# Two wide products first, then two narrow ones, in the weights-stationary projections of a decoder trunk

## The chip, the cores and the metric

The kernel runs on one core of a Trainium2 chip. The metric is device time in microseconds; the time before is the median of three runs. A profiled execution of the same program gives the trace that is read below.

The engines have the names of the profile: PE is the matrix engine (PEld its weight loads, which overlap its products), DVE and ACT are the two engines that work on whole tiles with 128 partitions, POOL and SP issue transfers here. A product (MATMUL) streams its moving operand, up to 512 columns, past a stationary one of 128 by 128 that a weight load (LDWEIGHTS) has put into PE before. It adds into an accumulator in PSUM. One PSUM tile of 128 partitions by 512 floats holds one accumulator.

## The reference

Four decoder layers on 256 tokens of 2048 features. Layer by layer the mixer is latent attention, sparse attention, sliding-window attention, and latent attention again. Each layer is one branch on a normalized input:

```
h = rmsnorm(x, norm_in[i])
self_out, mq, gate = mixer(h, w_in, ...)          # h @ w_in gives all streams
mem_out = memory_attention(mq, mem_n @ w_mem_kv[i])
y = concat(self_out, mem_out) * silu(gate)
x = x + y @ w_out[i]
```

and a last RMSNorm follows. All arrays are float32. Nearly all the arithmetic is in the products with weights: `w_in` (2048 by some 6700 to 7200), `w_mem_kv` (2048 by 2048), `w_out` (3072 by 2048), and in the latent layers `w_uq` and `w_ukv`.

## The kernel before

**High and low parts.** PE takes the operands in a rounded float32 form. To keep accuracy each operand is held as a high part, rounded, and a low part, the remainder. A product then is the sum of high times high, high times low and low times high. Activations are split once when they are made: `xT`, `cT` and `mT` hold for each block of 128 features a tile of 2 x 256 columns, the high parts of 256 tokens and then the low ones. Weights are split as they arrive: `stage` (L200) loads a tile `wr` with SP, and `parts_of` (L216) makes `wh` on ACT (the copy at L60) and `wl` on DVE (the subtraction at L64), 512 columns at a time, three buffers each.

**Two ways to multiply.** `rows_by` (L222) has the activations stationary and streams the weights: per weight row (128 features) and block of 128 tokens three products of up to 512 columns, L234 to L236. It makes values, the query and key streams that need rows, and the output projection. `columns_by` (L239), the function that is changed, has the weights stationary: the result comes out transposed, features on partitions. It works on 256 output features at a time, as two tiles `acc[0]` and `acc[1]` of 2 x 256 columns. Per weight row `kt` and tile `j` there are two products. The wide one (L253) has `wh` stationary and streams the high and the low part of the activations, 512 columns, over the whole accumulator. The narrow one (L255) has `wl` stationary and streams the high part alone, 256 columns, over the first half of the same accumulator. The halves are added when the accumulator is read: by `total` (L259) or `head_parts` (L265), with ACT and DVE.

A pair of `wh` and `wl` holds two weight rows (`k` is 0 or 1) of 256 columns, so eight products use one pair. A group, that is one call, has 16 weight rows for the input projections (`acc_g` gates, `acc_mq` memory queries, `acc_cq` the low-rank queries) and for the memory keys (`acc_mk`), 12 for `acc_qn` and 4 for `acc_kn`. PSUM holds four accumulators for products with weights (tag "acc"), so the group after next writes over the accumulators of this one.

**What sets the order.** The kernel is written for a planner: each engine's instructions are put into a fixed sequence beforehand by a plan that goes through the program with modelled durations. An instruction earlier in the program goes first, unless what it needs is not ready in the plan; then a later one that is ready takes its place. The sequence on PE therefore follows the source in general, with products of the attention of the previous part in between, and differs where an operand comes late in the plan. On the chip the engines run these fixed sequences and wait for each other with semaphores.

Memory keys and values of all four layers come first (up to some 400 us), then the four layers; in each the projections of one part are interleaved with the attention and the output projection of the part before.

Of the kernel before, what the change touches and what calls it, by code (L numbers as in the profile page):

```python
# [15 lines left out]
P = 128  # L16
S = 256
# [14 lines left out]
def kernel(ctx: ExitStack, tc: tile.TileContext, a: dict, out: bass.AP,  # L32
# [167 lines left out]
    def stage(w, k0, m, cols):  # L200

        n = cols[1] if len(cols) == 2 else cols[1] * cols[4]
        wr = wp.tile([P, ST * 512], F32, name="wr", tag="wr", bufs=WR)
        src = w[k0 * P:(k0 + m) * P, :].rearrange("(k p) n -> p k n", p=P)
        dst = wr[:, :m * n].rearrange("p (k n) -> p k n", k=m)
        if len(cols) == 2:
            nc.sync.dma_start(dst, src[:, :, cols[0]:cols[0] + n])
        else:
            c0, r, step, off, width = cols
            for k in range(m):  # L210
                nc.sync.dma_start(dst[:, k, :].rearrange("p (r c) -> p r c", r=r),
                                  src[:, k, c0:c0 + r * step].rearrange("p (r c) -> p r c", r=r)
                                  [:, :, off:off + width])
        return wr, n

    def parts_of(wr, c0, n):  # L216
        wh = wp.tile([P, 512], F32R, name="wh", tag="wh", bufs=3)
        wl = wp.tile([P, 512], F32R, name="wl", tag="wl", bufs=3)
        split(wh[:, :n], wl[:, :n], wr[:, c0:c0 + n])
        return wh, wl  # L220
# [18 lines left out]
    def columns_by(xt, kts, w, k0, cols, name):  # L239

        acc = [ps.tile([P, 2, S], F32, name=f"acc_{name}{j}", tag="acc", bufs=4) for j in range(2)]
        for s in range(0, kts, 2 * ST):
            m = min(2 * ST, kts - s)
            wr, n = stage(w, k0 + s, m, cols)
            for k2 in range(0, m, 2):
                wh, wl = parts_of(wr, k2 * S, 2 * S)
                for k in range(2):
                    kt = s + k2 + k
                    q = xt[kt // 4]
                    first, last = kt == 0, kt == kts - 1  # L250
                    for j in range(2):
                        o = k * S + j * P
                        nc.tensor.matmul(acc[j], wh[:, o:o + P], q[:, :, kt % 4, :],  # L253
                                         start=first, stop=False)
                        nc.tensor.matmul(acc[j][:, 0, :], wl[:, o:o + P], q[:, 0, kt % 4, :],  # L255
                                         start=False, stop=last)
        return acc

    def total(acc, name="z"):  # L259
# [47 lines left out]
    def memory():  # L307
# [19 lines left out]
        for i in range(depth):  # L327
            w = a["w_mem_kv"][i]
            for p_ in range(2):
# [11 lines left out]
                for h in (2 * p_, 2 * p_ + 1):  # L341
                    acc = columns_by(mT, 16, w, 0, (h * 256, 256), "mk")
                    kT = act.tile([P, 2, 2, S], F32R, name="mkT", tag="pq", bufs=PQ)
                    for j in range(2):
                        z = total(acc[j])
                        zs = wk.tile([P, S], F32, name="zs", tag="z", bufs=3)
                        nc.vector.tensor_mul(zs, z, mbc)
                        split(kT[:, 0, j, :], kT[:, 1, j, :], zs)
                    nc.gpsimd.dma_start(mkT[i][h], kT)
# [22 lines left out]
    def gate(nm, w, c0):  # L372
        gT = act.tile([P, 4, S], F32, name="gT", tag="gT", bufs=2)
        for h in range(2):
            acc = columns_by(nm.at, 16, w, 0, (c0 + h * S, S), "g")
            for j in range(2):
                z = total(acc[j])
                hz = wk.tile([P, S], F32, name="hz", tag="z", bufs=3)
                nc.vector.tensor_mul(hz, z, nm.half)
                th = wk.tile([P, S], F32, name="th", tag="e", bufs=4)  # L380
                nc.scalar.activation(th, hz, AF.Tanh)
                nc.vector.scalar_tensor_tensor(gT[:, 2 * h + j, :], th, 1.0, hz, op0=OP.add, op1=OP.mult)
        return gT
# [65 lines left out]
    def memory_project(nm, i, w, mq0, g0, part):  # L449
        kT, qT = [], []  # L450
        v = [act.tile([P, 2, 512], F32R, name="mvr", tag="aux", bufs=AUX) for z in range(2)]
        for z in range(2):
            nc.gpsimd.dma_start(v[z], mv[i][part][:, z])
        for h in range(2):
            k = act.tile([P, 2, 2, S], F32R, name="mkr", tag="pq", bufs=PQ)
            nc.gpsimd.dma_start(k, mkT[i][2 * part + h])
            kT.append(k)
            acc = columns_by(nm.at, 16, w, 0, (mq0 + part * 512 + h * 256, 256), "mq")
            q = act.tile([P, 2, 2, S], F32R, name="mqT", tag="pq", bufs=PQ)
            head_parts(q, acc)  # L460
            qT.append(q)
        return nm, kT, v, qT, gate(nm, w, g0 + 2048 + part * 512)
# [435 lines left out]
```

## Time and profile before

| | |
|---|---|
| Median of 3 runs | 2647.21 us (2645.34 to 2647.49) |
| Profiled execution | 2644.4 us, its span 2642.5 us |
| PE busy | 2614.7 us, 14623 products |
| PEld busy | 2268.1 us, 14623 weight loads |
| DVE busy, ACT busy | 1900.3 us, 1627.2 us |
| Mean granted PE clock | 0.998 |

The span goes from the first to the last instruction of the profiled execution. Busy is the union of an engine's instructions. Products overlap, each begins before the one ahead has ended, so what a product costs is read as the step from its start to the next one's start, not as its duration. The product rows L253 and L255 are those of the changed function.

### The profile page before, as it was taken

How to read it: one execution, taken by the hardware profiler on the slowest of the kernel's cores; microseconds unless marked ns; L12 is line 12 of the kernel's file. 1: busy time of each engine (PE TensorE's matmuls, PEld its weight loads, DVE VectorE, ACT ScalarE, POOL GpSimd, SP SyncE). 2: the span in 40 equal slices, each digit the busy share in tenths (PEclk: the TensorE clock that was granted, in tenths of full speed). 3: DMA queues.
4: the chain of work that ended last, by engine and by line, in shares of the span. 5: the costliest groups of instructions: out<-in, count | busy, mean ns of one | idle time of the engine just before them, and what ended most of it. 6: DMA issues, size and time to landing. Idle time of an engine off the chain costs nothing.

```text
span 2642.5 us, 43005 instructions
## 1 busy us (share of the span) xinstructions
PE 2614.7 (99%) x14623; PEld 2268.1 (86%) x14623; DVE 1900.3 (72%) x4174; ACT 1627.2 (62%) x3460; POOL 57.8 (2%) x102
## 2 busy tenths in 40 slices
PE   8999999999999999999999999999999999999998
PEld 7788888888888888888888888888888888888886
DVE  7566656677777786877777776777778767777767
ACT  6455556566656566666666666666666656665555
POOL 1000000000000000000000000000000000000000
PEclk9999999999999999999999999999999999999999
DMA  7888887565557655555556565555555756655763
GB/s 266 273 269 270 278 262 209 160 191 161 171 164 216 191 191 168 170 184 173 172 166 193 189 191 177 169 175 180 189 166 164 203 163 188 165 170 153 224 184 134
DMA packets 454065, 507.51 MB, mean 192 GB/s; under 512 B 69300, under 2 KB 352180, under 8 KB 452692
## 3 DMA queue, kind: packets, MB, share of 16 engines
q1 hardware_dynamic: 439716, 446.42, 55.5%
q0 software_dynamic: 13120, 56.17, 6.7%
q8 instruction: 115, 1.88, 0.3%
q10 hardware_dynamic: 1008, 2.16, 0.2%
q14 instruction: 106, 0.87, 0.1%
HBM read 485.70 MB, written 31.56 MB: 196 GB/s over the span
## 4 chain that ended last, share of the span: by engine, by line
PE 97%; DMA 2%; DVE 1%; ACT 0%; issue 0%; ACTq 0%; POOLq 0%
PE acc_g L253 14%; PE acc_g L255 7%; PE acc_wo L234 7%; PE acc_wo L235 7%; PE acc_wo L236 7%; PE acc_mq L253 5%; PE acc_mk L253 5%; PE acc_qn L253 3%; PE acc_cq L253 3%; PE acc_mq L255 2%; PE acc_mk L255 2%; PE acc_q L234 2%; PE acc_q L235 2%; PE acc_q L236 2%; PE acc_mv L235 2%; PE acc_mv L234 2%
## 5 line engine op out<-in xcount | busy, mean ns | idle before, releaser
L64 DVE TENSOR_TENSOR wl<-wr,wh 128x512 fp32r<-128x512 f32 (+2 forms) x1776 | 1171.6, 663 | 609.7 <-ACT wh L60 577.7
L60 ACT ACTIVATE wh<-wr 128x512 fp32r<-128x512 f32 (+2 forms) x1776 | 1080.5, 609 | 809.6 <-PE acc_g L253 172.4
L253 PE MATMUL acc_g<-xT,wh 128*128 128x512 f32 x1536 | 518.8, 398 | 0.0
L255 PE MATMUL acc_g<-xT,wl 128*128 128x256 f32 x1536 | 374.2, 282 | 0.0
L255 PEld LDWEIGHTS acc_g<-xT,wl 128*128 128x128 f32 x1536 | 287.5, 189 | 28.0
L235 PE MATMUL acc_wo<-wl,y 128*128 128x512 f32 x768 | 303.6, 395 | 0.8 <-DVE wl L64 0.8
L236 PE MATMUL acc_wo<-wh,y 128*128 128x512 f32 x768 | 298.6, 390 | 0.0
L253 PEld LDWEIGHTS acc_g<-xT,wh 128*128 128x128 f32 x1536 | 265.2, 188 | 36.4
L234 PE MATMUL acc_wo<-wh,y 128*128 128x512 f32 x768 | 240.7, 393 | 0.6 <-ACT wh L60 0.6
L253 PE MATMUL acc_mq<-xT,wh 128*128 128x512 f32 x512 | 173.2, 397 | 0.0
L253 PE MATMUL acc_mk<-mT,wh 128*128 128x512 f32 x512 | 171.4, 397 | 0.0
L235 PEld LDWEIGHTS acc_wo<-wl,y 128*128 128x128 f32 x768 | 144.3, 188 | 29.7 <-DVE wl L64 1.6
L236 PEld LDWEIGHTS acc_wo<-wh,y 128*128 128x128 f32 x768 | 144.3, 188 | 27.9
L234 PEld LDWEIGHTS acc_wo<-wh,y 128*128 128x128 f32 x768 | 141.7, 188 | 28.9 <-ACT wh L60 0.8
L805 DVE TENSOR_TENSOR x<-x,acc_wo 128x512 f32<-128x512 f32 x192 | 126.2, 681 | 12.3 <-PE acc_wo L236 12.1
L253 PE MATMUL acc_qn<-cT,wh 128*128 128x512 f32 x384 | 129.6, 398 | 0.0
L253 PE MATMUL acc_cq<-xT,wh 128*128 128x512 f32 x384 | 127.8, 395 | 0.0
L255 PE MATMUL acc_mq<-xT,wl 128*128 128x256 f32 x512 | 126.5, 285 | 0.0
L255 PE MATMUL acc_mk<-mT,wl 128*128 128x256 f32 x512 | 123.0, 282 | 0.0
L255 PEld LDWEIGHTS acc_mk<-mT,wl 128*128 128x128 f32 x512 | 96.6, 189 | 10.8
L235 PE MATMUL acc_q<-wl,xT 128*128 128x512 f32 x256 | 102.4, 400 | 0.0
L235 PE MATMUL acc_mv<-wl,mT 128*128 128x512 f32 x256 | 100.8, 394 | 0.3 <-DVE wl L64 0.3
(284 smaller groups left out, 4533.9 us busy)
## 6 DMA issues: line engine op xcount, KB each, us to landing
wr<-in_w_out_dram SPq DMA_DIRECT2D x192, 512.0 KB, 3.7
wr<-in_w_in_a_dram SPq DMA_DIRECT2D x176, 512.0 KB, 3.8
wr<-in_w_mem_kv_dram SPq DMA_DIRECT2D x128, 512.0 KB, 4.7
wr<-in_w_in_b_dram SPq DMA_DIRECT2D x112, 512.0 KB, 3.4
wr<-in_w_in_c_dram SPq DMA_DIRECT2D x104, 512.0 KB, 3.5
wr<-in_w_uq_dram SPq DMA_DIRECT2D x288, 128.0 KB, 2.7
tab<-flat POOLq DMA_DIRECT2D x8, 1536.0 KB, 11.0
wr<-in_w_in_a_dram SPq DMA_DIRECT2D x32, 288.0 KB, 3.2
```

What stands on the lines that cost most here:

```text
L60: nc.scalar.activation(o, i, AF.Copy, scale=scale)
L64: nc.vector.tensor_sub(lo, src, f32(hi))
L234: nc.tensor.matmul(acc[t][:, :n], xh, wh[:, :n], start=first, stop=False)
L235: nc.tensor.matmul(acc[t][:, :n], xh, wl[:, :n], start=False, stop=False)
L236: nc.tensor.matmul(acc[t][:, :n], xl, wh[:, :n], start=False, stop=last)
L253: nc.tensor.matmul(acc[j], wh[:, o:o + P], q[:, :, kt % 4, :], start=first, stop=False)
L255: nc.tensor.matmul(acc[j][:, 0, :], wl[:, o:o + P], q[:, 0, kt % 4, :], start=False, stop=last)
L805: nc.vector.tensor_add(xs, xs, acc[t])
```

## The change

Before, the two products of the first tile (wide, narrow) were written ahead of the two of the second tile (wide, narrow). After, the wide products of both tiles are written first and then both narrow ones. Operands, accumulators and the number of instructions are the same. The `start` and `stop` flags stay with the first wide and the last narrow product of each accumulator.

```diff
                 for k in range(2):
                     kt = s + k2 + k
                     q = xt[kt // 4]
-                    first, last = kt == 0, kt == kts - 1
+
                     for j in range(2):
                         o = k * S + j * P
                         nc.tensor.matmul(acc[j], wh[:, o:o + P], q[:, :, kt % 4, :],
-                                         start=first, stop=False)
+                                         start=kt == 0, stop=False)
+                    for j in range(2):
+                        o = k * S + j * P
                         nc.tensor.matmul(acc[j][:, 0, :], wl[:, o:o + P], q[:, 0, kt % 4, :],
-                                         start=False, stop=last)
+                                         start=False, stop=kt == kts - 1)
```

## The prediction

> **What bounds the kernel now.** I read the page first (span, busy shares, the chain that ended last), then the waits of PE, then the groups of instructions, and last the timeline of PE.
>
> ```profile
> span 2642.5 us, 43005 instructions
> PE 2614.7 (99%) x14623; PEld 2268.1 (86%) x14623; DVE 1900.3 (72%) x4174; ACT 1627.2 (62%) x3460; POOL 57.8 (2%) x102
> PE 97%; DMA 2%; DVE 1%; ACT 0%; issue 0%; ACTq 0%; POOLq 0%
> ```
>
> PE is busy for 99% of the span and carries 97% of the chain, so the time is the sum of the steps from one product's start to the next one's start. The waits of PE say how much of it is something else; the columns are who waited, for what, the total in us, how often, and the longest.
>
> ```profile
> PE gp L91 <- DMA rows<-in_mem_norm_dram: 7.6, 1, 7.6
> PE acc_mv L234 <- ACT wh L60: 3.2, 2, 2.9
> PE acc_kvb L234 <- ACT wh L60: 2.3, 1, 2.3
> PE acc_wo L235 <- DVE wl L64: 0.8, 2, 0.5
> ```
>
> Beside the first load (7.6 us) PE waits for 3.2 + 2.3 + 0.8 us and two smaller rows. Neither the splits nor the transfers set the pace. So the change is worth what it does to the step between products, and nothing else unless it makes a new wait.
>
> The groups give the number of products it touches. L253 is the 512-column product (I write W, wide), L255 the 256-column one (N, narrow):
>
> ```profile
> L253 PE MATMUL acc_g<-xT,wh 128*128 128x512 f32 x1536 | 518.8, 398 | 0.0
> L253 PE MATMUL acc_mq<-xT,wh 128*128 128x512 f32 x512 | 173.2, 397 | 0.0
> L253 PE MATMUL acc_mk<-mT,wh 128*128 128x512 f32 x512 | 171.4, 397 | 0.0
> L253 PE MATMUL acc_qn<-cT,wh 128*128 128x512 f32 x384 | 129.6, 398 | 0.0
> L253 PE MATMUL acc_cq<-xT,wh 128*128 128x512 f32 x384 | 127.8, 395 | 0.0
> L253 PE MATMUL acc_kn<-cT,wh 128*128 128x512 f32 x128 | 44.3, 397 | 0.0
> ```
>
> 1536 + 512 + 512 + 384 + 384 + 128 = 3456 wide products, and as many narrow ones. A weight row takes two of each, a quad: 1728 quads. The means of 398 ns are not steps: the products overlap, and what one costs has to be read from start to start.
>
> That is in the timeline of PE: start, length of the merged row, and "x2" where two products of one kind stand next to each other. The first stretch is an early one, the second is the last of the run:
>
> ```profile
> 44.35 0.64 PE L253 MATMUL acc_mk<-mT,wh 128*128 128x512 f32 x2
> 44.83 0.40 PE L255 MATMUL acc_mk<-mT,wl 128*128 128x256 f32 x2
> 45.06 0.40 PE L253 MATMUL acc_mk<-mT,wh 128*128 128x512 f32 x1
> ...
> 45.76 0.62 PE L253 MATMUL acc_mk<-mT,wh 128*128 128x512 f32 x2
> ...
> 2578.32 0.40 PE L253 MATMUL acc_g<-xT,wh 128*128 128x512 f32 x1
> 2578.55 0.28 PE L255 MATMUL acc_g<-xT,wl 128*128 128x256 f32 x1
> 2578.67 0.40 PE L253 MATMUL acc_g<-xT,wh 128*128 128x512 f32 x1
> 2578.91 0.28 PE L255 MATMUL acc_g<-xT,wl 128*128 128x256 f32 x1
> 2579.03 0.62 PE L253 MATMUL acc_g<-xT,wh 128*128 128x512 f32 x2
> 2579.49 0.40 PE L255 MATMUL acc_g<-xT,wl 128*128 128x256 f32 x2
> 2579.72 0.40 PE L253 MATMUL acc_g<-xT,wh 128*128 128x512 f32 x1
> ```
>
> The reader is to see that the source says W N W N, and yet every second quad of the program already runs as W W N N. I read it so: the planner took the second wide product where the low part wl was not ready in its plan: that is the first row of each pair of weight rows; in the second row of the pair both parts are there and the order is the written one. At 2579.03 the W W N N quad takes 0.69 us (to 2579.72), the W N W N quad before it 0.71 (2578.32 to 2579.03). Over the whole timeline I counted 620 undisturbed W W N N quads (those that start at 44.35 and 2579.03 are the first and the last), of mean 695.6 ns, and 790 undisturbed W N W N quads, of mean 707.8 ns. Counted with the disturbed ones, 815 quads have their two wide products side by side, 913 have not.
>
> **The change part by part.** It removes and adds no instruction, no transfer and no wait: 3456 products of each kind, 6912 weight loads and all the splits stay. Three things move.
>
> *The order in a quad.* 913 quads go from 707.8 to 695.6 ns: 913 x 12.2 ns = 11.1 us, all on PE and all on the path. The unknown in it: in the trace no two W W N N quads stand next to each other, each has a W N W N one before it. The rows that bound the pace of W W N N in an unbroken row are these, long runs of one kind and long runs of the alternating order:
>
> ```profile
> 700.66 0.62 PE L234 MATMUL acc_wo<-wh,y 128*128 128x512 f32 x2
> 702.02 0.62 PE L234 MATMUL acc_wo<-wh,y 128*128 128x512 f32 x2
> ...
> 2182.28 0.28 PE L235 MATMUL acc_qr<-wl,cT 128*128 128x256 f32 x1
> 2182.88 0.40 PE L253 MATMUL acc_qn<-cT,wh 128*128 128x512 f32 x1
> ...
> 895.33 0.40 PE L253 MATMUL acc_mq<-xT,wh 128*128 128x512 f32 x1
> 898.86 0.64 PE L253 MATMUL acc_mq<-xT,wh 128*128 128x512 f32 x2
> ...
> 1148.81 0.39 PE L253 MATMUL acc_g<-xT,wh 128*128 128x512 f32 x1
> 1150.55 0.62 PE L253 MATMUL acc_g<-xT,wh 128*128 128x512 f32 x2
> ```
>
> Six wide products of the rows loop take 702.02 - 700.66 = 1.36 us, 227 ns each; five narrow ones 0.60 us, 120 ns each. A quad made of these is 2 x (227 + 120) = 694 ns. The alternating order runs ten pairs in 3.53 us at 895.33 (706 ns a quad), but five pairs in 1.74 us at 1148.81 (696 ns). So there are two paces, some 694 and some 707 to 713, and the same order is found at both. The slow one is met by 641 of the 790 alternating quads and by 30 of the 620 others, of which 44.35 to 45.06 is one, at 0.71 us. Bounds for the new order: 693 ns below (the fastest quads of either order), 713 above. I take 695.6, since 589 of 620 quads of this order have it within 5 ns, whatever came before them.
>
> A page would have it otherwise. The Trainium skill, "TensorE: Matmul & The Clock Gate", section "Back-to-back issue gap", gives a warm step of N/2.4 + 2.5 ns, hence an estimate of 2 x (215.8 + 109.2) = 650 ns for a quad in any order, and a change worth 0 us. The trace disagrees with it on both counts, with 0.69 and 0.71 us for the two orders; it stays as a rival below.
>
> *The end of a group.* After sixteen weight rows (twelve, or four) the two accumulators are read out. The first was complete before the last W N; now it is complete one wide product later, 0.23 us. ACT and DVE, which read it, start 0.23 us later, and the splits queued behind those reads on both engines may shift with them. The accumulator is written again by the group after next, a whole group of some 11 us (16 x 702 ns) later where it has 16 rows. The short key groups are the place without such cover:
>
> ```profile
> 738.62 0.41 DVE L271 TENSOR_TENSOR qn<-zl,acc_qn 128x256 fp32r<-128x256 f32 x1
> ...
> 739.02 0.40 PE L253 MATMUL acc_kn<-cT,wh 128*128 128x512 f32 x1
> ```
>
> The last read of acc_qn ends at 739.03 and the wide product into that buffer starts at 739.02: released just in time. There are 8 such pairs of groups, and the value group behind each I count as just as near. At 16 places by at most 0.23 us this costs 3.7 us; below nothing it can't go, since nothing is freed earlier. I take 0.8 us, about a quarter, as the planner may put a narrow product first where the second accumulator is late.
>
> *When the parts come free.* The last use of wh in a pair moves ahead by one narrow product, 0.12 us, so ACT may begin the split after next by so much earlier; wl is freed as before. PE waits for splits in a few rows above only, so this is worth 0. No queue is passed: SP and POOL issue what they issued, by the same releases. The gain of the first 400 us, about 128 quads x 12.2 ns = 1.6 us, could be eaten by the waits for loads in that stretch (3.2 and 2.3 us above) if those end at a fixed time; I take 0, as the loads are released by PE's own progress, and keep 1.6 for the range.
>
> Sum: 11.1 - 0.8 = 10.3 us. The profiled execution took 2644.4 us (span 2642.5), so 2634.1, or 0.9961 of it. The median of the three runs, 2647.21, is 2.8 us above the profiled one; times 0.9961 it is 2636.9.
>
> **The rivals.** All quads together now average (815 x 695.6 + 913 x 707.8) / 1728 = 702.0 ns, and 0.2% of the time, about what a measurement of this kernel can tell from no change, is 5.3 us or 3.1 ns a quad.
>
> *The order does nothing.* The two paces belong to a state of PE's pipeline, not to the order: 1148.81 shows the written order at 696 ns, 44.35 the new one at 710. At 44.35 the slow W W N N is followed by a fast W N W N (45.06 to 45.76 in the same view), so that the eight products take the same 1.41 us as those from 2578.32 to 2579.72 (1.40). The 567 undisturbed eights of this kind, of which these are the first and, shifted by a quad, the last, have a mean of 1405.4 ns, 555 of them between 1400 and 1410. If eight products cost that whatever their order, a quad stays at 702 and the time at 2647. The same comes out if the planner kept its old order. Against it: 589 of 620, and 641 of 790. The skill's formula above would also end here.
>
> *Slower.* W W N N quads in an unbroken row lock into the slow pace, as the alternating ones do at 895.33. The price is in the row at 44.35: 713 ns for each of 1728 quads, 1728 x (713 - 702.0) = 19 us, 2666. It decides from a mean above 705.1. For it: the case was never seen, and what comes before a quad does matter in 30 of 620. Against it: the runs of one kind at 227 and 120 ns have no slow pace.
>
> **How the numbers follow.** My forecast has 0.70, with a range of its own of 2632 to 2641.9: below from 693 ns a quad (1728 x 9 = 15.6 us less), above the 0.2% bound, which 3.7 us at the group ends and 1.6 us of the early stretch still leave (11.1 - 5.3 = 5.8). No change has 0.16, slower 0.14. The range for all reaches from 2631 into the case of no change, to 2649, which leaves about 2 in 10 out, most of it the slower case.
>
> **What would show it.** In the changed kernel's timeline nearly every weight row should read "L253 x2", "L255 x2", and one such quad should take 0.69 to 0.70 us from start to start; a full gate group, 16 quads of which 8 change, should fall by about 0.1 us. PE's waits should stay below 10 us beside the first load. If the quads read 0.70 to 0.71 in an unbroken row, the order alone was not the cause; if the order is right and the quads are fast but the time is not down by 10 us, the loss is in new waits for ACT or DVE at acc_kn and acc_va, or for loads before 400 us.

## The result, and the profile after

The changed kernel takes 2637.05 us (median of 6 runs) against 2646.06 us before (median of 6): a ratio of 0.9964, with a 95% interval from 0.9954 to 0.9974. Measured once more later, beside another experiment, the ratio was 0.9975 (0.9965 to 0.9984). So 0.25 to 0.36% went, some 6 to 10 us; the two intervals together allow 0.16 to 0.46%. The prediction had 2636.9 us; its sum, 10.3 us, is at the upper end of that, and the reason it gave for it was only half right.

The profiled execution has a span of 2635.0 us, 7.5 less than before. From the page of the changed kernel:

```profile
span 2635.0 us, 43048 instructions
PE 2605.1 (99%) x14623; PEld 2260.1 (86%) x14623; DVE 1890.2 (72%) x4174; ACT 1625.5 (62%) x3460; POOL 57.8 (2%) x102
```

PE still sets the time, with the same 14623 products. The waits of PE in the changed kernel (who, for what, us in total, times, longest):

```profile
PE gp L91 <- DMA rows<-in_mem_norm_dram: 7.2, 1, 7.2
PE acc_kvb L234 <- ACT wh L60: 1.8, 1, 1.8
PE o L786 <- ACT pT L60: 1.7, 3, 0.6
PE acc_mk L253 <- ACT wh L60: 1.4, 1, 1.4
PE ptp L402 <- ACT e L60: 1.4, 3, 0.5
```

The waits have mostly moved: the 3.2 us at acc_mv are nearly gone, and 1.4 us at acc_mk and 3.1 us in the attention (o, ptp) have come. All rows behind the first load make some 9 us now and 7 before. There is no wait at acc_kn, where the prediction had looked for one.

The timeline of PE, in a gate group of the changed kernel (L257 is the narrow product here):

```profile
743.48 0.63 PE L253 MATMUL acc_g<-xT,wh 128*128 128x512 f32 x2
743.95 0.39 PE L257 MATMUL acc_g<-xT,wl 128*128 128x256 f32 x2
744.18 0.62 PE L253 MATMUL acc_g<-xT,wh 128*128 128x512 f32 x2
...
747.66 0.63 PE L253 MATMUL acc_g<-xT,wh 128*128 128x512 f32 x2
```

Every quad now reads "x2", "x2". Six of them take 747.66 - 743.48 = 4.18 us, 696.7 ns each. Counted over the whole trace, 1359 undisturbed quads (with products of this function ahead of them, behind them and throughout) run in this order, of mean 697.0 ns. 68 quads still alternate, 32 of them in acc_kn, where the planner has kept W N W N. A full gate group takes 11.14 us now and took 11.25.

I added up the steps from each product's start to the next one's. The wide and narrow products of `columns_by` take 1216.34 us after and 1223.57 before: 7.2 us less. All other products take 1398.1 us after and 1397.9 before, but only in the sum. Part by part they moved both ways: acc_mv takes 3.5 us less and acc_wo 1.8 less, o takes 3.2 us more and ptp 2.8 more. These shifts come with the new plan; they stand within 0.6 us in the second profile of the changed kernel, and they cancel. What is left of the difference lies in the changed products, as a shorter step.

### The profile page after: what moved, and what is told of

Read it like the earlier page. It is cut to its first block, busy times and chain, and to the rows that moved or that the text cites. A ratio compares the mean times of both kernels' runs of the same rounds, so it can differ in the third digit from the quotient of the medians.

```text
span 2635.0 us, 43048 instructions
## 1 busy us (share of the span) xinstructions
PE 2605.1 (99%) x14623; PEld 2260.1 (86%) x14623; DVE 1890.2 (72%) x4174; ACT 1625.5 (62%) x3460; POOL 57.8 (2%) x102
## 4 chain that ended last, share of the span: by engine, by line
PE 97%; DMA 1%; DVE 1%; ACT 0%; issue 0%; ACTq 0%; POOLq 0%
PE acc_g L253 14%; PE acc_g L257 7%; PE acc_wo L234 7%; PE acc_wo L235 7%; PE acc_wo L236 7%; PE acc_mq L253 5%; PE acc_mk L253 5%; PE acc_qn L253 3%; PE acc_cq L253 3%; PE acc_mq L257 2%; PE acc_mk L257 2%; PE acc_q L234 2%; PE acc_q L235 2%; PE acc_q L236 2%; PE acc_mv L235 2%; PE acc_mv L236 2%
## 5 line engine op out<-in xcount | busy, mean ns | idle before, releaser
L253 PE MATMUL acc_g<-xT,wh 128*128 128x512 f32 x1536 | 488.9, 397 | 0.6 <-DVE z L264 0.6
L257 PEld LDWEIGHTS acc_g<-xT,wl 128*128 128x128 f32 x1536 | 285.2, 188 | 60.7
L257 PE MATMUL acc_g<-xT,wl 128*128 128x256 f32 x1536 | 311.0, 280 | 0.0
L253 PEld LDWEIGHTS acc_g<-xT,wh 128*128 128x128 f32 x1536 | 238.1, 189 | 4.7 <-issue 1.1
L253 PE MATMUL acc_mk<-mT,wh 128*128 128x512 f32 x512 | 160.8, 396 | 1.4 <-ACT wh L60 1.4
L253 PE MATMUL acc_mq<-xT,wh 128*128 128x512 f32 x512 | 161.7, 397 | 0.0
L253 PE MATMUL acc_qn<-cT,wh 128*128 128x512 f32 x384 | 123.2, 399 | 0.0
L253 PE MATMUL acc_cq<-xT,wh 128*128 128x512 f32 x384 | 120.8, 396 | 0.0
L257 PEld LDWEIGHTS acc_mk<-mT,wl 128*128 128x128 f32 x512 | 95.8, 188 | 22.7 <-DVE wl L64 0.4
L257 PEld LDWEIGHTS acc_mq<-xT,wl 128*128 128x128 f32 x512 | 93.7, 188 | 20.0
L257 PE MATMUL acc_mq<-xT,wl 128*128 128x256 f32 x512 | 102.5, 281 | 0.0
L257 PE MATMUL acc_mk<-mT,wl 128*128 128x256 f32 x512 | 100.8, 278 | 0.0
```

## The experiments

The theory on record was that each quad (four products of one weight row) has a price by its own order: 707.8 ns alternating, 695.6 two and two. Its rival was that the two paces are a state of PE, with eight products at 1405 ns in any order. Two more could be named as reasons for a price by order: each change of width costs, or each product that writes the accumulator its predecessor has just written costs.

### Alternating everywhere

```diff
-                        nc.tensor.matmul(acc[j], wh[:, o:o + P], q[:, :, kt % 4, :],
-                                         start=first, stop=False)
+                        wide = nc.tensor.matmul(acc[j], wh[:, o:o + P], q[:, :, kt % 4, :],
+                                                start=first, stop=False)
+                        if j == 1:
+                            tc.keep_in_program_order(wide)
```

This is the kernel before, with the second wide product of a row pinned behind the first narrow one.

> The order of before, but each second wide product is pinned behind the first narrow one, so that the planner can't put two wide products side by side: nearly all 1728 quads run W N W N. If the order of widths sets the pace (707.8 ns for W N W N, 695.6 for W W N N in the trace of before), the 815 quads that stood as W W N N lose 12.2 ns each: 9.9 us, 2656 us, ratio to before about 1.0038. If the two paces are a state of PE and eight products cost 1405 ns in any order, the time stays at 2646 (ratio 1.000) and the quads average 702. If an unbroken alternating order finds the fast pace (694, as at 1148.81 us in the trace of before), the kernel is faster than before: 1728 x 8 ns = 14 us, 2632.

Measured: 2645.99 us against 2645.36, a ratio of 1.0004 (0.9995 to 1.0013). Hardly a quad is two and two any more, and yet nothing is lost. The undisturbed quads have a mean of 702.7 ns, but that is a mean of long stretches at one of two paces. (A single quad of the slow stretches takes 711 or 699 ns, so a pace has to be read over many.) From the timeline of PE in this kernel, the ends of two stretches of 15 quads each:

```profile
88.42 0.40 PE L253 MATMUL acc_mk<-mT,wh 128*128 128x512 f32 x1
...
99.02 0.40 PE L253 MATMUL acc_mk<-mT,wh 128*128 128x512 f32 x1
...
2570.13 0.39 PE L253 MATMUL acc_g<-xT,wh 128*128 128x512 f32 x1
...
2580.53 0.39 PE L253 MATMUL acc_g<-xT,wh 128*128 128x512 f32 x1
```

The first takes 10.60 us, 706.7 ns a quad, the second 10.40 us, 693.3, with a granted clock of 1.00 in both. So the alternating order has no price of its own: it is the fastest order or a slow one. The theory on record falls in this form; the 707.8 ns were those of alternating quads behind a W W N N.

### The narrow products in the other order

```diff
-                    for j in range(2):
+                    for j in (1, 0):
                         o = k * S + j * P
                         nc.tensor.matmul(acc[j][:, 0, :], wl[:, o:o + P], q[:, 0, kt % 4, :],
```

> The changed kernel with the two narrow products of a row exchanged: W0 W1 N1 N0. The widths follow each other as in the changed kernel, but twice in a quad a product goes into the accumulator that the one ahead of it has just written (W1 N1, and N0 before the next W0), as it did in W N W N. If the change of width is what costs, quads stay at 697 ns and the time at 2637 (ratio 0.9965). If writing the same accumulator twice running is what costs, quads go to about 708 and the time to about 2656 (ratio 1.004).

Measured: 2637.83 us, ratio 0.9973 (0.9963 to 0.9982), undisturbed quads of mean 697.0 ns, as in the changed kernel. Which accumulator the product before has written makes no difference.

### Four and four

```diff
-                for k in range(2):
-                    kt = s + k2 + k
-                    q = xt[kt // 4]
...
+                for part in range(2):
+                    for k in range(2):
+                        kt = s + k2 + k
+                        q = xt[kt // 4]
+                        for j in range(2):
+                            o = k * S + j * P
+                            if part == 0:      # the wide product, else the narrow one
```

> All four wide products of a pair of weight rows first, then its four narrow ones: half as many changes of width as in the changed kernel. If each change of width costs, quads come down from 697 towards 694 ns, the sum of long runs of one kind (227 and 120 ns): up to 5 us less than the changed kernel, 2632 to 2635, ratio 0.9945 to 0.996, unless the later narrow products make new waits at the group ends (then above 2637). If the pace of the changed kernel is a floor of PE with this operand stream, quads stay at 697 and the time at 2637.

Measured: 2648.93 us, ratio 1.0016 (1.0007 to 1.0025): slower than before, and 11 us slower than the mirrored kernel on the same chip. From the timeline of PE:

```profile
748.78 1.09 PE L254 MATMUL acc_g<-xT,wh 128*128 128x512 f32 x4
749.71 0.64 PE L257 MATMUL acc_g<-xT,wl 128*128 128x256 f32 x4
750.19 1.09 PE L254 MATMUL acc_g<-xT,wh 128*128 128x512 f32 x4
```

Two quads take 1.41 us here; the 578 undisturbed eights have a mean of 1401.8 ns, 700.9 a quad. Fewer changes of width did not help: half as many as in the changed kernel, and 4 ns a quad more. That would be 6.7 us of the 11 for 1728 quads. In the sums of steps the changed products take 5.8 us more than in the mirrored kernel, and all others 5.7 more, of which 3.4 are longer waits at o (3.9 us for ACT and 1.2 for DVE, against 1.7). The rest of the others is not explained.

### PE alone

The two paces of one order could still come from the work beside PE. This kernel keeps PE alone: tiles loaded and split once, and then runs of 24 quads in each order, with transposes ahead of each run.

```
for rep in range(6):
    for order in ("alt", "two", "mir", "four", "wide", "narrow", "one"):
        turn(5 + rep)                       # 5 to 10 transposes
        for p in range(12):                 # two weight rows each, always the same tiles
            if order == "alt":
                for k, kt in ((0, t0), (1, t1)):
                    W(k, 0, kt), N(k, 0, kt), W(k, 1, kt), N(k, 1, kt)
            elif order == "two":
                for k, kt in ((0, t0), (1, t1)):
                    W(k, 0, kt), W(k, 1, kt), N(k, 0, kt), N(k, 1, kt)
            ...
```

> Not the kernel: it loads one tile of weights and one of activations, splits them once, and then runs the products of seven orders on PE alone, 24 quads of each, six times over, with five to ten transposes ahead of each run; the rest of the computation is left out and the output is the input plus a sum of accumulators. No semaphore is waited for inside a run, and ACT and DVE are idle but for reading the accumulators. Steps from start to start, for a quad: if the order of widths sets the pace, alternating 706 to 712, two and two 695 to 698, mirrored the same as two and two, four and four 694 to 696, wide alone 227 to 229 per product, narrow alone 119 to 120, alternating in one accumulator 706 to 712. If the same accumulator twice running costs, mirrored is like alternating, and alternating in one accumulator slower still. If the slow pace is made by the work of ACT and DVE or by waits between them and PE, all orders run at 694 here.

From the timeline of PE in this run, the first product of the third quad and the first product behind the last quad, for three runs (22 quads lie between the two):

```profile
13.96 0.39 PE L83 MATMUL acc_alt<-xT,wh 128*128 128x512 f32 x1
...
29.21 0.39 PE L83 MATMUL acc_alt<-xT,wh 128*128 128x512 f32 x1
...
121.61 0.40 PE L83 MATMUL acc_alt<-xT,wh 128*128 128x512 f32 x1
...
137.16 0.40 PE L83 MATMUL acc_alt<-xT,wh 128*128 128x512 f32 x1
...
139.68 0.40 PE L83 MATMUL acc_two<-xT,wh 128*128 128x512 f32 x1
...
155.01 0.40 PE L83 MATMUL acc_two<-xT,wh 128*128 128x512 f32 x1
```

Alternating took 15.25 us in the first place (693 ns a quad) and 15.55 in the second (707): both paces, on the same tiles, with ACT and DVE idle and a granted clock of 1.00 in both stretches. Of its six runs five were fast and one slow. Two and two took 15.33 us (697) in all six, mirrored as well, four and four took 701 to 702 ns a quad. Alternating in one accumulator was at 707 four times and at 693 twice. Wide products alone took 226.7 to 226.9 ns each, narrow ones alone 120.0, so the fast alternating pace is just their sum, 2 x (226.7 + 120.0) = 693.4, and the other orders pay some ns on top. The paces are PE's own. Which of the two an alternating run takes differed from place to place in the program; two and two has but one.

### The same with the splits beside it

```diff
             for j in range(2):
                 nc.vector.tensor_add(res, res, acc[j].rearrange("p a b -> p (a b)"))
+            side(24)                        # 24 splits on ACT and DVE
```

> As the quiet run with ACT and DVE splitting one weight tile over and over beside it, so that both are busy nearly all the time; the rest left out. If the paces belong to PE alone: the same as in the quiet run, alternating 694 or 707, two and two 696, mirrored 696, four and four 701. If reads of weights by PE contend with the splits: all orders slower by some ns a product, and alternating no longer at 694 anywhere.

Measured: with DVE busy for 93% and ACT for 86% of this run, two and two is at 697 in all six places, mirrored at 697, four and four at 701, and alternating settles at 693 or 707. Eleven of the twelve alternating runs (in two accumulators and in one) even took the same pace as in the run before, so the choice is not chance; it goes with the place in the program, and what about the place decides is open. The work of ACT and DVE adds nothing to these paces. (The span is longer, 712.0 us against 678.0, but that is the splits left over at the end: from PE's first product to its last it is 662.2 us here and 661.2 there.)

### All cyclic orders

There are ten cyclic orders of four wide and four narrow products. One of them, w w n n w n w n, is what the planner had made of the kernel before.

> As the quiet run, PE alone on fixed tiles, the rest of the computation left out: all ten cyclic orders of four wide and four narrow products, 24 quads each, five times over with five to nine transposes ahead. From the quiet run: two and two 696 ns a quad whatever comes ahead, alternating 694 or 707, four and four 701. The order of the planner before (w w n n w n w n, two quads) is the one that decides between theories: if each quad has a price by its own order it should take 695 + 694 or 707, so 694.5 or 701 on average, depending on what came ahead; if eight products lock into one pace of their own, it takes 1405 to 1407 ns (703 a quad) each time, with nothing on ACT and DVE. If any order stays below 696 in all five places, it is a candidate for a kernel that beats both.

From the timeline of PE in this run, again 22 quads between the two rows of each:

```profile
103.43 0.40 PE L83 MATMUL acc_wwnwnwnn<-xT,wh 128*128 128x512 f32 x1
...
118.97 0.40 PE L83 MATMUL acc_wwnwnwnn<-xT,wh 128*128 128x512 f32 x1
...
156.92 0.40 PE L83 MATMUL acc_wwnnwnwn<-xT,wh 128*128 128x512 f32 x1
...
172.39 0.40 PE L83 MATMUL acc_wwnnwnwn<-xT,wh 128*128 128x512 f32 x1
```

The planner's old order takes 15.47 us, 703.3 ns a quad, in all five places; two and two 696.7, in all five; w w n w n w n n 15.54 us, 706.7, in all five. w n w n w n w n was at 693.3 three times and at 706.7 twice. The other orders, left out here, keep paces from 698.6 to 706.7. The number of changes of width does not sort them: w w n w w n n n, with four changes as in two and two, takes 706.6, and w w n w n n w n, with six, takes 700.0. (The first runs of the first two orders are not counted: the order was not kept there.) No order stays below 696.7 everywhere, so none is a candidate for a faster kernel.

So on PE alone a rhythm of eight products locks into a pace that belongs to the whole sequence. The order of the change and that of the kernel before differ there by 703.3 - 696.7 = 6.6 ns a quad.

### An order that must be slow

If that is right, an order with the same changes of width as before, but with the pace 706.7, must lose in the kernel.

```diff
+                for wide, k, j in ((1, 0, 0), (1, 0, 1), (0, 0, 0), (1, 1, 0), (0, 0, 1), (1, 1, 1),
+                                   (0, 1, 0), (0, 1, 1)):
```

> The changed kernel with the eight products of a pair of weight rows in the order w w n w n w n n, which took 706.7 ns a quad in all five places of the run on PE alone, against 703.3 for w w n n w n w n, the planner's order in the kernel before, and 696.7 for two and two. Both have six changes of width in eight products. If the locked pace of an order carries over to the kernel: 10 ns a quad above the changed kernel, 3.4 above before; with 0.8 to 1 of the 1728 quads undisturbed, 14 to 17 us above the changed kernel and 5 to 6 above before, 2650 to 2652, ratio 1.002. If the number of changes of width counted, it would be equal to before, 2645.

Measured: 2651.35 us, ratio 1.0026 (1.0016 to 1.0036). The changed kernel, on the same chip beside it:

> The changed kernel once more, on the same chip as the run beside it: ratio 0.996 to 0.997, 2637. Undisturbed quads at 696.7 ns, as in the run on PE alone.

Measured: 2638.29 us, ratio 0.9975 (0.9965 to 0.9984). The two differ by 13.1 us in the medians and in the spans (2649.2 and 2636.1), and PE waits in nearly the same places in both. From the timeline of PE in the slow kernel:

```profile
749.03 0.63 PE L253 MATMUL acc_g<-xT,wh 128*128 128x512 f32 x2
749.50 0.28 PE L256 MATMUL acc_g<-xT,wl 128*128 128x256 f32 x1
749.61 0.40 PE L253 MATMUL acc_g<-xT,wh 128*128 128x512 f32 x1
749.84 0.28 PE L256 MATMUL acc_g<-xT,wl 128*128 128x256 f32 x1
749.96 0.40 PE L253 MATMUL acc_g<-xT,wh 128*128 128x512 f32 x1
750.20 0.40 PE L256 MATMUL acc_g<-xT,wl 128*128 128x256 f32 x2
...
753.27 0.63 PE L253 MATMUL acc_g<-xT,wh 128*128 128x512 f32 x2
```

Six quads take 753.27 - 749.03 = 4.24 us, 706.7 ns each, 10 more than in the changed kernel. The 13.1 us are 0.76 of 1728 x 10 ns, a little below the 0.8 to 1 that was expected; 11.2 of them are in the steps of the changed products. Against before the slow kernel loses 6.7 us, a little more than the 5 to 6 expected. The paces found on PE alone carry over to the kernel, and the number of changes of width does not decide.

### The width of the narrow product

What makes the rhythm? The nearest suspect was the weight load, which begins with the product ahead of it (within 6 ns of its start in the other runs on PE alone), and which a narrow product might just fail to cover. To go above 256 columns, the narrow product streams equal pieces of the high and the low part here; at 256 columns it gave the same paces as before, 693 or 707 and 697.

> As the quiet run, PE alone on fixed tiles, the rest left out: alternating (alt) and two and two (two) with the narrow product at 192, 256, 288, 320 and 384 columns (letters a to e), four times over. The theory under test: a weight load that begins with the product ahead of it is just not covered by a narrow product of 256 columns (113 ns of streaming at 0.443 ns a column, the pace of the wide one), so that the wide one behind it waits some ns for its weights, and that wait locks into a rhythm that depends on the order. It expects at 192 columns (85 ns of streaming) narrow steps still at 112 to 120 ns; at 288 and above steps of 0.443 ns a column and no difference between alt and two (a quad of 708, 737 and 794 ns at 288, 320 and 384). The rival, that the rhythm comes with every change of width or from the clocks and not from the load, expects narrow steps of about 85 to 90 ns at 192, and a difference between alt and two at 288 to 384 columns as well.

From the timeline of PE in this run: the two ends of 22 quads at 320 columns, alternating and two and two, and then three successive products at 192, with the weight loads (PEld) that start beside them.

```profile
121.48 0.39 PE L84 MATMUL acc_altd<-xT,wh 128*128 128x512 f32 x1
...
138.05 0.39 PE L84 MATMUL acc_altd<-xT,wh 128*128 128x512 f32 x1
...
140.57 0.39 PE L84 MATMUL acc_twod<-xT,wh 128*128 128x512 f32 x1
...
157.00 0.39 PE L84 MATMUL acc_twod<-xT,wh 128*128 128x512 f32 x1
...
201.11 0.42 PE L84 MATMUL acc_alta<-xT,wh 128*128 128x512 f32 x1
201.37 0.25 PE L92 MATMUL acc_alta<-xT,wl 128*128 128x192 f32 x1
201.46 0.42 PE L84 MATMUL acc_alta<-xT,wh 128*128 128x512 f32 x1
...
201.14 0.19 PEld L92 LDWEIGHTS acc_alta<-xT,wl 128*128 128x128 f32 x1
201.37 0.19 PEld L84 LDWEIGHTS acc_alta<-xT,wh 128*128 128x128 f32 x1
201.48 0.19 PEld L92 LDWEIGHTS acc_alta<-xT,wl 128*128 128x128 f32 x1
```

At 192 columns the step of the narrow product is 0.09 us (201.37 to 201.46; 87 to 90 ns in this run), not 112 to 120. But the wide product ahead of it then takes 0.26 us in place of 0.23, so the pair costs 31 ns more than 704 columns at 0.443. The loads show why: the one at 201.48 begins 0.02 us behind its product, at 201.46. Inside the runs of products on PE alone no load starts less than 107 ns behind the load ahead. At 192 columns the load that begins with the wide product comes 21 to 25 ns late and keeps that distance, and by about as much the wide step has grown. I read it so that the loads do hold PE up at 192 columns, and that the pair has the floor which the theory wanted in the narrow step. At 256 columns and above every load begins within 6 ns of its product, in every order. From 288 columns on the theory had no difference between the orders. But at 320 columns alternating takes 753 ns a quad (16.57 us) and two and two 747 (16.43): a difference of 6.6 the same way as in the kernel. At 288 it is the other way, 720 and 727, and at 384 both take 826 to 827; the theory had 737 for 320, 708 for 288 and 794 for 384. At 192 two and two has two paces as well, 680 and 689. The theory of the uncovered load falls as the reason for the paces: the order still matters at 288 and 320 columns, and no load is late there or at the kernel's 256. That the load plays no part at all is not shown. What sets the paces stays open.

The Trainium skill, "TensorE: Matmul & The Clock Gate", section "LDWEIGHTS (loading the stationary operand)", has a load take the number of columns divided by 1.2 ns, by which a load of 128 columns is estimated at 107 ns, longer than the step of 87 to 90 ns at 192 columns. The trace agrees as far as the spacing goes: at 192 columns successive loads start 108 ns apart at the least, though each is on record for 187 to 192 ns or more. It doesn't hold for every load: in the changed kernel some loads behind a transpose follow the one ahead after 82 ns.

## Why the prediction was right or wrong

*What bounds the kernel.* Right. PE's steps set the time before and after, and the difference of the sums of steps of the changed products, 7.2 us, is nearly the difference of the spans, 7.5.

*The order in a quad, 913 x 12.2 ns = 11.1 us.* The direction was right, the term was too large, and the reasoning behind it failed at one step. It took 695.6 and 707.8 ns for prices of the two kinds of quad, and so only the 913 alternating quads were to gain. The runs put in its place: the planner's mixture locks as a whole, at 703.3 ns a quad on PE alone, two and two at 696.7, and alternating by itself at 693.3 or 706.7. So the quads that stood as W W N N lost a little (695.6 to about 697), the alternating ones gained nearly 11. By the counted means, (815 x 695.6 + 913 x 707.8) / 1728 = 702.0 before and 697.0 after, the gain is 5.0 x 1728 = 8.6 us; 7.2 were measured in the steps of these products, with 68 quads that still alternate, and the wait of 1.4 us at acc_mk, in between.

*The bounds of the unseen case.* Two W W N N quads side by side had not been seen; 693 to 713 was allowed and 695.6 taken. It is 696.7 in every run of it on PE alone, and 697.0 in the kernel. Taking the sum of 227 and 120 ns as the nearest row (694) would have been too fast by 2.7 ns, which is 4.7 us here.

*The end of a group, 0.8 us.* Not there. At acc_kn the planner kept W N W N in the eight later groups, and PE waits for nothing at acc_kn. Instead waits came in the attention (o and ptp, 3.1 us) and went at acc_mv: the plan as a whole had shifted. That the first median lies within 0.2 us of 2636.9 is luck in part. With three more runs the median before went from 2647.21 to 2646.06, and the two medians differ by 9.0 us, not 10.3; the second measurement, 0.9975, puts the gain at 6.6 us, and the steps of the trace at 7.2.

*When the parts come free, and the first 400 us.* The 0 us is right only on balance. The same 1871 products up to the last one of acc_mk end at 376.2 us now and at 381.5 before, 5.3 us sooner: 3.5 at acc_mv (the wait there went from 3.2 to below 1), 1.3 in the steps of acc_mk, though a wait of 1.4 came there, and 0.5 from an earlier first load. The attention gave back 6.0 us later, at o and ptp. The prediction had no term for either.

*The rival of no change* was half right. In place of "the order does nothing", which 0.9964 and 0.9975 rule out, what holds is: alternating everywhere costs the same as the mixture (1.0004), for it is fast in some stretches and slow in others. The prediction had the right rows for it, 1148.81 and 895.33.

*The slower rival* had the right mechanism, an order that locks into the slow pace, and the wrong order: w w n w n w n n does it (1.0026), two and two doesn't.

*The signs.* All came true: nearly every row in the new order, 0.69 to 0.70 us for a quad, 0.1 us less for a gate group, some 9 us of waits beside the first load. They could not tell a price for each quad from a pace of the whole sequence; the alternating kernel did.

The formula for a warm step in the Trainium skill, "TensorE: Matmul & The Clock Gate", section "Back-to-back issue gap", which the page calls the isolated gap, would give 650 ns for a quad in any order, by estimate; the runs gave 693 to 707 by order, so the measurement decides against it for this kind of product and load.

## What to carry to other kernels

Where PE is the bound and every product has its own weight load, the order of products of unlike width can be worth 1% of those products with no change in any count (13.1 us of some 1220 between the slow kernel and the changed one). What it is worth is read from the steps between starts over a long stretch of exactly the order that will run; a pace read from a mixture is that of the mixture. Look first at what order the planner has made, since it may not be the source's, and measure candidate orders on PE alone: a run of under a millisecond gave the paces that the kernel then showed.

## What the runs showed of the hardware

On fixed tiles, with nothing waited for, the step between products cycles through a few values some 3.3 ns apart (226 to 227, 230, 233, 236, 240 ns for 512 columns, clearest in the run of all cyclic orders) and locks into a cycle. The locked paces of a quad, 693.3, 696.7, 700.0, 703.3, 706.7 and, with other widths, 720.0, 726.7, 746.7, 753.3 and 826.7, are whole multiples of 3.33 ns; a few others (698.6 and 701.3, and 688.9 at 192 columns) are not. I had not expected that one order can hold two paces for as long as it runs, 693.3 and 706.7 ns for W N W N. The granted clock was 1.00 in both of the stretches shown, so the throttle does not explain it. Loads of 128 columns ahead of these products start no closer than 107 ns to each other on PE alone; at 192 columns that seems to be what bounds the pair, and at 256 no load is late. Why a sequence locks where it does, and how to bring an alternating run to its fast pace (it would be worth 3.4 ns a quad against two and two, an estimate of 5.9 us for all 1728), is open.
